# RMS norm with gelu: the squares, the gelu and the store of one group in a row on ScalarE

## The chip, the cores and the metric

The kernel runs on one core of one Trainium2 chip. The metric is device time in microseconds (us) of one execution, as the median of several. The profile is of one execution; its span is from the first to the last instruction.

Four engines matter: ScalarE (ACT in the profile; squares, gelu, and issue of the stores), VectorE (DVE; the product with gamma), GpSimd (POOL; the inverse root) and SyncE (SP; issue of the loads). TensorE only spreads gamma over the partitions at the start.

## The reference

```python
# x: 8 x 1024 x 2048, gamma: 2048, all float32
rms = np.sqrt(np.mean(x ** 2, axis=-1, keepdims=True) + eps)
out = gamma * x / rms
return 0.5 * out * (1 + np.tanh(np.sqrt(2 / np.pi) * (out + 0.044715 * out ** 3)))
```

The input is 67.1 MB, the output as much.

## The kernel before

The 8192 rows are cut into 16 groups; a group gives each of 128 partitions four rows, 4.19 MB in all. Six buffers ("slots") hold groups. A group is loaded into a slot, changed in place, and stored from it; the load of group g + 6 needs the store of group g to be done.

```python
ROWS = 4
SLOTS = 6
...
store_pieces = {G - 1: [(0, 2), (2, 2)]}
scale_pieces = {G - 1: [(0, 1), (1, 1), (2, 1), (3, 1)]}
...
def squares(g):                      # ScalarE, 4 x [128, 2048], sum per row
    for r in range(R):
        nc.scalar.activation(out=junk, in_=slot[g % SLOTS][:, r, :],
                             func=ACT.Square, accum_out=ssq[:, g, r : r + 1])

def scale(g):                        # VectorE, rows *= gamma
    for r, n in scale_pieces.get(g, [(0, R)]):
        rows = slot[g % SLOTS][:, r : r + n, :]
        nc.vector.tensor_tensor(out=rows, in0=rows, in1=gamma_ps..., op=ALU.mult)

def inverse_rms(g):                  # GpSimd, six small instructions -> rstd
    ...

def gelu_store(g):                   # ScalarE: gelu(rstd * row), then the store
    for r, n in store_pieces.get(g, [(0, R)]):
        for q in range(r, r + n):
            nc.scalar.activation(out=row, in_=row, func=ACT.Gelu_apprx_tanh,
                                 scale=rstd[:, g, q : q + 1])
        nc.scalar.dma_start(out=o3[g, :, r : r + n, :], in_=...)
...
for g in range(G + 1):
    if g < G:
        squares(g)
        inverse_rms(g)
        scale(g)
    if g:
        gelu_store(g - 1)
        if g - 1 + SLOTS < G:
            load(g - 1 + SLOTS)
```

The loop is shifted by one: ScalarE does the squares of group g, and then the gelu of group g - 1, whose scale and inverse root were made meanwhile by the other engines.

Of the kernel before, what the change touches and what calls it, by code (L numbers as in the profile page):

```python
# [1 line left out]

# [4 lines left out]

FP32 = mybir.dt.float32
ALU = mybir.AluOpType
ACT = mybir.ActivationFunctionType  # L10

P = 128
ROWS = 4
SLOTS = 6

GW = 128


@with_exitstack
def kernel(  # L20
    ctx: ExitStack,
    tc: tile.TileContext,
    x: bass.AP,
    gamma: bass.AP,
    eps: bass.AP,
    out: bass.AP,
):




    nc = tc.nc
    D = x.shape[-1]
    R = ROWS
    eps_f = float(eps)
    x3 = x.rearrange("b s d -> (b s) d").rearrange("(g p r) d -> g p r d", p=P, r=R)
    o3 = out.rearrange("b s d -> (b s) d").rearrange("(g p r) d -> g p r d", p=P, r=R)
    G = x3.shape[0]

    sbuf = ctx.enter_context(tc.tile_pool(name="sbuf", bufs=1))  # L40
    psum = ctx.enter_context(
        tc.tile_pool(name="psum", bufs=1, space=bass.MemoryType.PSUM)
    )
    slot = [sbuf.tile([P, R, D], FP32, name=f"slot{i}") for i in range(SLOTS)]
    gamma_row = sbuf.tile([1, D // GW, GW + 16], FP32, name="gamma_row")
    ones = sbuf.tile([1, P], FP32, name="ones")
    warm = sbuf.tile([1, 1], FP32, name="warm")
    power = sbuf.tile([P, R], FP32, name="power")
    ssq = sbuf.tile([P, G, R], FP32, name="ssq")
    rstd = sbuf.tile([P, G, R], FP32, name="rstd")  # L50
    ms = sbuf.tile([P, R], FP32, name="ms")
    y = sbuf.tile([P, R], FP32, name="y")
    z = sbuf.tile([P, R], FP32, name="z")
    gamma_ps = psum.tile([P, D], FP32, name="gamma_ps")
    junk = psum.tile([P, D], FP32, name="junk")

    store_pieces = {G - 1: [(0, 2), (2, 2)]}
    scale_pieces = {G - 1: [(0, 1), (1, 1), (2, 1), (3, 1)]}

    def load(g):  # L60
        nc.sync.dma_start(out=slot[g % SLOTS], in_=x3[g])  # L61

    def squares(g):
        for r in range(R):
            nc.scalar.activation(  # L65
                out=junk,
                in_=slot[g % SLOTS][:, r, :],
                func=ACT.Square,
                accum_out=ssq[:, g, r : r + 1],
            )  # L70

    def scale(g):
        for r, n in scale_pieces.get(g, [(0, R)]):
            rows = slot[g % SLOTS][:, r : r + n, :]
            nc.vector.tensor_tensor(  # L75
                out=rows,
                in0=rows,
                in1=gamma_ps.unsqueeze(1).to_broadcast([P, n, D]),
                op=ALU.mult,
            )  # L80

    def inverse_rms(g):

        v = nc.gpsimd
        v.tensor_scalar(  # L85
            out=ms, in0=ssq[:, g, :], scalar1=1.0 / D, scalar2=eps_f,
            op0=ALU.mult, op1=ALU.add,
        )
        v.tensor_tensor(out=y, in0=ms, in1=power, op=ALU.pow)  # L89
        v.tensor_tensor(out=z, in0=y, in1=y, op=ALU.mult)  # L90
        v.tensor_tensor(out=z, in0=z, in1=ms, op=ALU.mult)  # L91
        v.tensor_scalar(  # L92
            out=z, in0=z, scalar1=-0.5, scalar2=1.5, op0=ALU.mult, op1=ALU.add
        )
        v.tensor_tensor(out=rstd[:, g, :], in0=z, in1=y, op=ALU.mult)  # L95

    def gelu_store(g):
        for r, n in store_pieces.get(g, [(0, R)]):
            for q in range(r, r + n):
                row = slot[g % SLOTS][:, q, :]  # L100
                nc.scalar.activation(  # L101
                    out=row, in_=row, func=ACT.Gelu_apprx_tanh,
                    scale=rstd[:, g, q : q + 1],
                )
            nc.scalar.dma_start(  # L105
                out=o3[g, :, r : r + n, :], in_=slot[g % SLOTS][:, r : r + n, :]
            )

    with tc.manual_schedule():
        for g in range(SLOTS):  # L110
            load(g)
        nc.scalar.dma_start(
            out=gamma_row[:, :, 0:GW],
            in_=gamma.rearrange("(o a b) -> o a b", o=1, b=GW),
        )
        nc.gpsimd.memset(power, -0.5)  # L116
        nc.vector.memset(warm, 0.0)  # L117
        nc.vector.memset(ones, 1.0)  # L118
        nc.scalar.activation(out=warm, in_=warm, func=ACT.Gelu_apprx_tanh)  # L119
        for k in range(0, D, 512):  # L120
            nc.tensor.matmul(  # L121
                out=gamma_ps[:, k : k + 512],
                lhsT=ones,
                rhs=gamma_row[:, k // GW : (k + 512) // GW, 0:GW],
                start=True,
                stop=True,
            )
        for g in range(G + 1):
            if g < G:
                squares(g)  # L130
                inverse_rms(g)
                scale(g)
            if g:
                gelu_store(g - 1)
                if g - 1 + SLOTS < G:
                    load(g - 1 + SLOTS)


# [1 line left out]
_INS = ['x', 'gamma', 'eps']  # L140
_OUTS = [((8, 1024, 2048), 'float32')]

_NUMBERS = {'eps': 9.999999747378752e-06}


# [26 lines left out]
```

## Time and profile before

| | before |
|---|---|
| time, median of 4 runs | 317.65 us |
| span of the profile (of an execution that took 318.66 us) | 316.9 us |
| ScalarE busy | 251.1 us (79%) |
| VectorE busy | 139.4 us (44%) |
| DMA, mean rate | 424 GB/s |
| ScalarE waits for loads | 43.7 us |
| ScalarE waits for VectorE or GpSimd | none |

The chain of the kernel before, that is, the work that ended last followed backwards to what released it, by engine and then by line, as shares of the span ("issue" is time in which the engine waited for nothing that the profile shows; ACTq and SPq are the instruction queues of ScalarE and SyncE, the issue of transfers above all):

```profile
DMA 56%; ACT 33%; issue 5%; ACTq 1%; SPq 0%
DMA slot<-in_x_dram 30%; DMA out_dram<-slot 26%; ACT slot L101 19%; ACT junk L65 14%; ACTq L105 1%; SPq L61 0%; ACTq L101 0%; ACTq L65 0%
```

More than half of this chain is transfers, loads and stores. No instruction of VectorE or GpSimd is in it.

### The profile page before, as it was taken

What the parts mean: (1) busy time and instruction counts of PE and PEld (TensorE: products, weight loads), DVE (VectorE), ACT (ScalarE), POOL (GpSimd) and SP (SyncE); (2) the same over time, 40 slices, a digit from 0 to 9 for tenths busy, and PEclk for the clock granted to TensorE, in tenths of its full rate; (3) what the DMA queues carried; (4) which work ended last, traced back from release to release, by engine and by line L of the source; (5) the groups of instructions that cost most, each with busy time, mean ns of one, the idle gap of its engine ahead of it and who ended that gap; (6) DMA issues with size and microseconds to landing.
All of it is one profiled execution on the core that took longest, in us unless ns stands there. A gap on an engine that the chain in (4) does not pass through costs nothing.

```text
span 316.9 us, 473 instructions
## 1 busy us (share of the span) xinstructions
PE 7.2 (2%) x8; PEld 2.5 (1%) x8; DVE 139.4 (44%) x21; ACT 251.1 (79%) x194; POOL 32.3 (10%) x101
## 2 busy tenths in 40 slices
PE   0900000000000000000000000000000000000000
PEld 0300000000000000000000000000000000000000
DVE  0038909090919191732808246091550905582000
ACT  1379999999999997959689595995959859599800
POOL 0020102020202020202002020020200102001000
DMA  8999999999999999999999999999999999999995
GB/s 328 414 451 426 434 393 459 401 459 402 459 405 455 426 434 431 430 434 426 438 426 455 410 455 418 443 426 430 434 430 435 422 459 405 459 414 447 422 420 230
DMA packets 4787, 134.25 MB, mean 424 GB/s; under 512 B 544, under 2 KB 560, under 8 KB 560
## 3 DMA queue, kind: packets, MB, share of 16 engines
q1 hardware_dynamic: 2304, 67.11, 49.5%
q10 hardware_dynamic: 2480, 67.12, 49.1%
q14 instruction: 3, 0.02, 0.0%
HBM read 67.12 MB, written 67.11 MB: 424 GB/s over the span
## 4 chain that ended last, share of the span: by engine, by line
DMA 56%; ACT 33%; issue 5%; ACTq 1%; SPq 0%
DMA slot<-in_x_dram 30%; DMA out_dram<-slot 26%; ACT slot L101 19%; ACT junk L65 14%; ACTq L105 1%; SPq L61 0%; ACTq L101 0%; ACTq L65 0%
## 5 line engine op out<-in xcount | busy, mean ns | idle before, releaser
L75 DVE TENSOR_TENSOR slot<-slot,gamma_ps 128x8192 f32<-128x8192 f32 (+1 forms) x19 | 139.2, 7340 | 147.0 <-ACT junk L65 147.0
L65 ACT ACTIVATE junk<-slot 128x2048 f32<-128x2048 f32 x64 | 120.4, 1881 | 47.3 <-DMA slot<-in_x_dram 43.7
L101 ACT ACTIVATE slot<-slot,rstd 128x2048 f32<-128x2048 f32 x64 | 122.8, 1989 | 0.9 <-ACT slot L101 0.9
L85 POOL TENSOR_SCALAR ms<-ssq 128x4 f32<-128x4 f32 x16 | 3.1, 194 | 247.5 <-ACT junk L65 247.5
L89 POOL TENSOR_TENSOR y<-ms,power 128x4 f32<-128x4 f32 x16 | 16.1, 1009 | 1.3
L65 ACT ACTIVATION_READ_ACCUMULATOR junk<-slot 128x1 f32 x64 | 12.0, 188 | 0.0
L121 PE MATMUL gamma_ps<-gamma_row,ones 1*128 1x512 f32 x8 | 7.2, 1072 | 8.4 <-DMA gamma_row<-in_gamma_dram 8.4
L95 POOL TENSOR_TENSOR rstd<-z,y 128x4 f32<-128x4 f32 x16 | 3.2, 201 | 1.3
L91 POOL TENSOR_TENSOR z<-z,ms 128x4 f32<-128x4 f32 x16 | 3.2, 201 | 1.3
L90 POOL TENSOR_TENSOR z<-y 128x4 f32<-128x4 f32 x16 | 3.2, 199 | 1.3
L92 POOL TENSOR_SCALAR z<-z 128x4 f32<-128x4 f32 x16 | 3.1, 194 | 1.4
L121 PEld LDWEIGHTS gamma_ps<-gamma_row,ones 1*128 1x128 f32 x8 | 2.5, 325 | 11.5 <-issue 11.5
L119 ACT ACT_TABLE_LOAD x1 | 1.3, 1283 | 1.3 <-PEq L153 1.3
L117 DVE MEMSET warm<- 1x1 f32 x1 | 0.1, 59 | 0.8 <-PEq L153 0.8
L119 ACT ACTIVATE warm<-warm 1x1 f32<-1x1 f32 x1 | 0.2, 202 | 0.0
L118 DVE MEMSET ones<- 1x128 f32 x1 | 0.2, 165 | 0.0
L116 POOL MEMSET power<- 128x4 f32 x1 | 0.1, 102 | 0.3 <-POOLq L153 0.3
L153 POOL MEMSET const-float32-0.0<- 128x1 f32 x1 | 0.1, 99 | 0.2 <-issue 0.2
L153 POOL MEMSET const-bfloat16-1.0<- 128x1 bf16 x1 | 0.1, 102 | 0.0
L153 POOL MEMSET const-uint8-127<- 128x1 uint8 x1 | 0.1, 102 | 0.0
L153 POOL MEMSET const-float32-1.0<- 128x1 f32 x1 | 0.1, 99 | 0.0
## 6 DMA issues: line engine op xcount, KB each, us to landing
slot<-in_x_dram SPq DMA_DIRECT2D x16, 4096.0 KB, 37.1
out_dram<-slot ACTq DMA_DIRECT2D x15, 4096.0 KB, 38.6
out_dram<-slot ACTq DMA_DIRECT2D x2, 2048.0 KB, 15.0
gamma_row<-in_gamma_dram ACTq DMA_DIRECT2D x1, 8.0 KB, 7.5
```

The costliest lines, as they stand in the source:

```text
L65: nc.scalar.activation(out=junk, in_=slot[g % SLOTS][:, r, :], func=ACT.Square, accum_out=ssq[:, g, r : r + 1],)
L75: nc.vector.tensor_tensor(out=rows, in0=rows, in1=gamma_ps.unsqueeze(1).to_broadcast([P, n, D]), op=ALU.mult,)
L85: v.tensor_scalar(out=ms, in0=ssq[:, g, :], scalar1=1.0 / D, scalar2=eps_f, op0=ALU.mult, op1=ALU.add,)
L89: v.tensor_tensor(out=y, in0=ms, in1=power, op=ALU.pow)
L90: v.tensor_tensor(out=z, in0=y, in1=y, op=ALU.mult)
L91: v.tensor_tensor(out=z, in0=z, in1=ms, op=ALU.mult)
L92: v.tensor_scalar(out=z, in0=z, scalar1=-0.5, scalar2=1.5, op0=ALU.mult, op1=ALU.add)
L95: v.tensor_tensor(out=rstd[:, g, :], in0=z, in1=y, op=ALU.mult)
L101: nc.scalar.activation(out=row, in_=row, func=ACT.Gelu_apprx_tanh, scale=rstd[:, g, q : q + 1],)
L105: nc.scalar.dma_start(out=o3[g, :, r : r + n, :], in_=slot[g % SLOTS][:, r : r + n, :])
L119: nc.scalar.activation(out=warm, in_=warm, func=ACT.Gelu_apprx_tanh)
L121: nc.tensor.matmul(out=gamma_ps[:, k : k + 512], lhsT=ones, rhs=gamma_row[:, k // GW : (k + 512) // GW, 0:GW], start=True, stop=True,)
```

## The change

The intent, as the code reads, is to finish a group at once: its squares, its gelu and its store follow each other on ScalarE, so that a slot is given back earlier. To keep the wait for the scale short, the scale is cut in two halves of two rows, each issued after the squares of its rows. This is done in groups 0 to 9 only, whose slots are used again; groups 10 to 15 have one scale of four rows. The finer pieces of the last group's scale and store go, and two memsets move from VectorE to GpSimd.

```diff
-    def scale(g):
-        for r, n in scale_pieces.get(g, [(0, R)]):
-            rows = slot[g % SLOTS][:, r : r + n, :]
+    def scale(g, r, n):
+        rows = slot[g % SLOTS][:, r : r + n, :]
...
-    def gelu_store(g):
-        for r, n in store_pieces.get(g, [(0, R)]):
+    def gelu(g):
+        for r in range(R):
...
+    def store(g):
+        nc.scalar.dma_start(out=o3[g], in_=slot[g % SLOTS])
...
-        nc.vector.memset(warm, 0.0)
-        nc.vector.memset(ones, 1.0)
+        nc.gpsimd.memset(warm, 0.0)
+        nc.gpsimd.memset(ones, 1.0)
...
-        for g in range(G + 1):
-            if g < G:
-                squares(g)
-                inverse_rms(g)
-                scale(g)
-            if g:
-                gelu_store(g - 1)
-                if g - 1 + SLOTS < G:
-                    load(g - 1 + SLOTS)
+        for g in range(G):
+            n = HALF if g < G - SLOTS else R      # HALF = 2
+            for r in range(0, R, n):
+                squares(g, r, n)
+                scale(g, r, n)
+            inverse_rms(g)
+            gelu(g)
+            store(g)
+            if g + SLOTS < G:
+                load(g + SLOTS)
```

More of the change, by code (lines that the diff above doesn't have):

```diff
@@ L14 @@
 SLOTS = 6
+HALF = 2
 GW = 128
@@ L55, with squares @@
     junk = psum.tile([P, D], FP32, name="junk")
-    store_pieces = {G - 1: [(0, 2), (2, 2)]}
-    scale_pieces = {G - 1: [(0, 1), (1, 1), (2, 1), (3, 1)]}
     def load(g):
         nc.sync.dma_start(out=slot[g % SLOTS], in_=x3[g])
-    def squares(g):
-        for r in range(R):
+    def squares(g, r, n):
+        for q in range(r, r + n):
             nc.scalar.activation(
                 out=junk,
-                in_=slot[g % SLOTS][:, r, :],
+                in_=slot[g % SLOTS][:, q, :],
                 func=ACT.Square,
-                accum_out=ssq[:, g, r : r + 1],
+                accum_out=ssq[:, g, q : q + 1],
             )
-    def scale(g):
-        for r, n in scale_pieces.get(g, [(0, R)]):
-            rows = slot[g % SLOTS][:, r : r + n, :]
-            nc.vector.tensor_tensor(
-                out=rows,
-                in0=rows,
-                in1=gamma_ps.unsqueeze(1).to_broadcast([P, n, D]),
-                op=ALU.mult,
-            )
+    def scale(g, r, n):
+        rows = slot[g % SLOTS][:, r : r + n, :]
+        nc.vector.tensor_tensor(
+            out=rows,
+            in0=rows,
+            in1=gamma_ps.unsqueeze(1).to_broadcast([P, n, D]),
+            op=ALU.mult,
+        )
     def inverse_rms(g):
@@ L95, in inverse_rms @@
         v.tensor_tensor(out=rstd[:, g, :], in0=z, in1=y, op=ALU.mult)
-    def gelu_store(g):
-        for r, n in store_pieces.get(g, [(0, R)]):
-            for q in range(r, r + n):
-                row = slot[g % SLOTS][:, q, :]
-                nc.scalar.activation(
-                    out=row, in_=row, func=ACT.Gelu_apprx_tanh,
-                    scale=rstd[:, g, q : q + 1],
-                )
-            nc.scalar.dma_start(
-                out=o3[g, :, r : r + n, :], in_=slot[g % SLOTS][:, r : r + n, :]
-            )
+    def gelu(g):
+        for r in range(R):
+            row = slot[g % SLOTS][:, r, :]
+            nc.scalar.activation(
+                out=row, in_=row, func=ACT.Gelu_apprx_tanh,
+                scale=rstd[:, g, r : r + 1],
+            )
+    def store(g):
+        nc.scalar.dma_start(out=o3[g], in_=slot[g % SLOTS])
     with tc.manual_schedule():
```

## The prediction

> **What bounds the kernel now.** I read four views in this order: the page (busy shares, transfer rate), the waits of ScalarE, the groups by form for durations, and the timeline of one group for the order on each engine.
>
> The page of the kernel before:
>
> ```profile
> PE 7.2 (2%) x8; PEld 2.5 (1%) x8; DVE 139.4 (44%) x21; ACT 251.1 (79%) x194; POOL 32.3 (10%) x101
> ...
> DMA  8999999999999999999999999999999999999995
> GB/s 328 414 451 426 434 393 459 401 459 402 459 405 455 426 434 431 430 434 426 438 426 455 410 455 418 443 426 430 434 430 435 422 459 405 459 414 447 422 420 230
> DMA packets 4787, 134.25 MB, mean 424 GB/s; under 512 B 544, under 2 KB 560, under 8 KB 560
> ```
>
> The DMA row is full from the second slice to the last but one. The transfers are the bound: 134.25 MB at 424 GB/s is the whole span of 316.9 us. No compute engine is above 79%. A group of 4 rows moves 4.19 MB in and 4.19 MB out; at the 433 GB/s that the windows between 80 and 240 us show, that is 19.4 us a group, and the timeline has the first squares of successive groups at 140.10, 159.44 and 178.78 us, 19.34 apart.
>
> The waits of ScalarE:
>
> ```profile
> ACT junk L65 <- DMA slot<-in_x_dram: 43.7, 11, 10.3
> ACT junk L65 <- ACT slot L101: 2.1, 5, 0.4
> ```
>
> ScalarE waits for loads (43.7 us), and never for VectorE or GpSimd: no such line is in the view. The slack is smaller than 21% idle suggests. Before about 119 us it has none: it works off the loads that came early, one group in 16.1 us. After that it has 3.7 us in each 19.34.
>
> The groups by form, then the timeline around group 0, the only place where a group's sums and its scale stand with nothing before them:
>
> ```profile
> L75 DVE TENSOR_TENSOR slot<-slot,gamma_ps 128x8192 f32<-128x8192 f32 x15 | 130.3, 8688 | 142.4 <-ACT junk L65 142.4
> L101 ACT ACTIVATE slot<-slot,rstd 128x2048 f32<-128x2048 f32 x64 | 122.8, 1989 | 0.9 <-ACT slot L101 0.9
> L65 ACT ACTIVATE junk<-slot 128x2048 f32<-128x2048 f32 x64 | 120.4, 1881 | 47.3 <-DMA slot<-in_x_dram 43.7 <-ACT slot L101 2.1
> L89 POOL TENSOR_TENSOR y<-ms,power 128x4 f32<-128x4 f32 x16 | 16.1, 1009 | 1.3
> ```
>
> ```profile
> 13.13 1.88 ACT L65 ACTIVATE junk<-slot 128x2048 f32<-128x2048 f32 x1 [10.29 <-DMA slot<-in_x_dram]
> ...
> 21.05 0.19 ACT L65 ACTIVATION_READ_ACCUMULATOR junk<-slot 128x1 f32 x1
> 21.27 8.69 DVE L75 TENSOR_TENSOR slot<-slot,gamma_ps 128x8192 f32<-128x8192 f32 x1 [20.27 <-ACT junk L65]
> 21.33 0.20 POOL L85 TENSOR_SCALAR ms<-ssq 128x4 f32<-128x4 f32 x1 [20.51 <-ACT junk L65]
> ...
> 22.91 1.88 ACT L65 ACTIVATE junk<-slot 128x2048 f32<-128x2048 f32 x1 [1.67 <-DMA slot<-in_x_dram]
> ...
> 23.55 0.20 POOL L95 TENSOR_TENSOR rstd<-z,y 128x4 f32<-128x4 f32 x1
> ...
> 30.93 7.67 ACT L101 ACTIVATE slot<-slot,rstd 128x2048 f32<-128x2048 f32 x4
> ...
> 38.62 0.36 ACTq L105 DMA_DIRECT2D out_dram<-slot  x1
> 39.03 1.88 ACT L65 ACTIVATE junk<-slot 128x2048 f32<-128x2048 f32 x1 [0.43 <-ACT slot L101]
> ```
>
> The reader is to see three things. Four squares take 13.13 to 21.24, 8.11 us. The scale follows 0.03 us later and takes 8.69; the inverse root ends at 23.75, 2.51 us after the squares. And ScalarE does the squares of group 1 (22.91 on) while VectorE scales group 0: that is what hides the 8.69 us.
>
> **What the Trainium skill says.** (1) "ScalarE: Activation LUTs", section "What ACT_TABLE_LOAD costs": an activation with immediate scale and bias takes 186 ns plus 0.833 ns an element, each pointer operand about 93 ns more, and back-to-back ones overlap by about 93 ns. At 2048 elements that is 1892 and 1985; the trace has 1881 and 1989, and four gelus in 7.67, so 1.89 apart. It agrees. (2) "VectorE: DVE Perf Modes", section on the TRN2 errata: a 32-bit tensor by tensor operation takes (N+151)/0.96 ns. For 8192 that is 8690, the trace has 8688. For the new 4096 form, which no row shows, it gives an estimate of 4.42 us. (3) "DMA: Bandwidth & Descriptors", section "Issuing engines are not separate DMA queues": transfers issued by different engines run on the same 16 DMA engines and interleave. The trace agrees: loads and stores share one 433 GB/s. (4) "Perfetto Trace Analysis", section "Optimization Strategy" under "Identifying Performance Opportunities": a kernel can have regimes with different limits. The trace shows that for this one (16.1 us a group of ScalarE first, 19.34 of DMA later), and I argue that the change makes a third.
>
> **The change part by part.** The compiled order of instructions shows the ScalarE stream as four squares, four gelus, store, group by group; the first gelu of a group waits for VectorE and GpSimd. Groups 0 to 9 have two scales of 128x4096, groups 10 to 15 one of 128x8192. ScalarE takes instructions in order, so a gelu that waits holds back the next group's squares.
>
> *Groups 0 to 9.* Squares 8.11. The first scale half runs beside squares 3 and 4 (4.42 against 4.07, it ends about 0.4 after them). The inverse root ends 2.51 after the squares; with about 0.08 for the signal the first gelu starts 2.59 after them. The second half queues behind the first, some 4.8 to 4.9 us after the squares; the third gelu would start at 2.59 + 3.79 = 6.4, so it waits for nothing. Four gelus 7.67, then 0.43 from the last gelu's end to the next squares (38.60 to 39.03). Sum 8.11 + 2.59 + 7.67 + 0.43 = 18.80 us of ScalarE a group.
>
> *Groups 10 to 15.* The one scale starts only after all four squares: 8.11 + 0.03 + 8.69 + 0.08 + 7.67 + 0.43 = 25.01 us.
>
> One small addition: the compiled program has the fourth gelu of each group wait on ScalarE's own semaphore, which it did not before. In the squares such a wait makes the next start 0.02 after the former ended instead of overlapping, so I allow 0.12: 18.9 and 25.1.
>
> *What lies beside other work.* 18.9 us is just under the 19.4 of the DMA, but the early loads are already there: the sixth load lands near 80 us before, while ScalarE starts group 5 only at 13.1 + 5 x 18.9 = 107.6. With reads and writes halving the DMA, a load lands each 19.4 us after the third, against 18.9 of use: the lead of 18 us shrinks by 0.5 a group and lasts through group 10. So ScalarE never waits for a load, and its chain sets the end: 13.13 (first load) + 10 x 18.9 + 6 x 25.1 = 352.7, less 0.4 for the issue in the sum, so the last store is issued near 352.3. The removed split of the last store counts too: the last 4.19 MB now go alone, nothing queued ahead. The first load took 12.4 us from issue to landing, the same size; 2.1 lie between the last landing and the end before (300.64 + 14.2 to 316.9). So span 352.3 + 12.4 + 2.1 = 366.8, and the timed median stands 1.0 above the profile's span (317.9 to 316.9): 367.8. I take 367.5.
>
> *The memsets* that move to GpSimd cost 0.2 us beside the 8.4 us wait for gamma: nothing.
>
> **The rivals.** (a) *The transfers still hide all.* The full DMA row and 21% idle on ScalarE speak for it, and stores go out earlier after their load. Against it: 16 groups of over 18.8 us serial work are at least 301 us plus 13 before and 14 after. This would be about 318. (b) *Only the length of 18.9 matters*, as if whole scales in the last six cost nothing because no slot is reused there: 13.1 + 16 x 18.9 + 14.5 + 1 = 331, slower by 4%. The compiled order speaks against it, since in-order gelus wait for the whole scale. (c) *The early gelu waits for both halves* through a coarse wait: first groups would take 8.11 + about 4.9 + 7.67 + 0.43 = 21.1 us, above the DMA's pace, and the end some 22 us later, 390. The compiled order has separate waits for gelu one and three, so it is unlikely. (d) *Store issues on ScalarE block* on a semaphore shared with an older transfer: the waits are on stores four groups back or on a load that landed long before; at worst a few us.
>
> **Range and chances.** The sum is of measured durations and the order is fixed; the doubts are 16 small gaps (0.1 each, 2 us), the lone last store (2 us) and the early groups (2 us). Range 362 to 373. Faster 0.01, same 0.02, slower 0.97.
>
> **What would show it.** The waits of ScalarE should have gelu on VectorE, about 6 x 8.8 = 53 us (last six), gelu on GpSimd, about 10 x 2.6 = 26 us, and for loads only the first 10 us. First squares should be 18.9 apart to group 10, then 25.1. The DMA row should thin out in the last third. If squares still wait for loads in the middle, the DMA share was misjudged and the time is longer in that stretch; if the last groups stand less than 20 us apart, the step on in-order waits is wrong and the time is near 331.

## The result, and the profile after

The changed kernel takes 363.8 us (median of 4 runs, 363.73 to 364.11) against 317.65 us for the kernel before in the same rounds. The ratio is 1.1443, with a 95% interval of 1.1402 to 1.1483: slower by 14%. Ratios here are the mean time of one kernel's fast runs over that of the other's of the same rounds, so not quite the ratio of the medians quoted.

The page of the changed kernel: busy time of the engines, then the busy share of the DMA in tenths and its rate in 40 slices of 9.05 us each.

```profile
PE 7.2 (2%) x8; PEld 2.5 (1%) x8; DVE 139.7 (39%) x26; ACT 252.5 (70%) x194; POOL 32.3 (9%) x103
...
DMA  8999999999999999999999999999998508209028
GB/s 345 409 460 402 413 445 424 442 427 434 435 431 438 427 442 417 453 413 449 413 456 413 453 416 453 416 453 416 445 421 351 232 0 348 116 29 434 0 116 348
DMA packets 4643, 134.25 MB, mean 371 GB/s; under 512 B 528, under 2 KB 544, under 8 KB 544
```

The engines do the same work as before: ScalarE 252.5 us against 251.1, VectorE 139.7 against 139.4. The bytes are the same too. What differs is the last quarter: for 30 slices the transfers run as before, and then they thin out, with whole slices idle. In the window from 40 to 200 us the changed kernel moved 433 GB/s, the one before 432. In the window from 201 to 351 us it moved 298.

The chain by engine, and the waits of ScalarE (engine and group, what it waited for: us in total, times, longest):

```profile
ACT 65%; DVE 14%; issue 6%; POOL 6%; DMA 3%; ACTq 1%
```

```profile
ACT slot L98 <- DVE slot L73: 52.9, 6, 8.8
ACT slot L98 <- POOL rstd L93: 25.2, 10, 2.5
ACT junk L64 <- DMA slot<-in_x_dram: 10.3, 1, 10.3
```

Of the transfers only 3% is left in the chain: the first load. VectorE and GpSimd are in it now. Before, ScalarE waited 43.7 us in 11 waits for loads and never for these two. Now it waits for one load only, the first, but 78.1 us for the two engines: six times 8.8 us for VectorE and ten times 2.5 us for GpSimd. Its idle time before did not go away; it was replaced by another wait and grew.

The timeline of group 1, one of the first ten (start, duration, engine, line, operation; in brackets the idle time before it and what ended it):

```profile
31.87 1.88 ACT L64 ACTIVATE junk<-slot 128x2048 f32<-128x2048 f32 x1 [0.43 <-ACT slot L98]
...
35.94 8.75 DVE L73 TENSOR_TENSOR slot<-slot,gamma_ps 128x4096 f32<-128x4096 f32 x2 [9.99 <-ACT junk L64]
...
39.79 0.19 ACT L64 ACTIVATION_READ_ACCUMULATOR junk<-slot 128x1 f32 x1
...
42.27 0.20 POOL L93 TENSOR_TENSOR rstd<-z,y 128x4 f32<-128x4 f32 x1
42.50 7.68 ACT L98 ACTIVATE slot<-slot,rstd 128x2048 f32<-128x2048 f32 x4 [2.52 <-POOL rstd L93]
50.21 0.34 ACTq L104 DMA_DIRECT2D out_dram<-slot  x1
50.59 1.88 ACT L64 ACTIVATE junk<-slot 128x2048 f32<-128x2048 f32 x1 [0.42 <-ACT slot L98]
```

From squares to squares it is 50.59 - 31.87 = 18.72 us. The scale halves end at 44.69, while the first two gelus run. What ScalarE waits for is the last of GpSimd's six instructions, which ends at 42.47. Compare the kernel before, where ScalarE went from the squares into the gelu of the former group without a gap.

The timeline of group 10, the first with a whole scale:

```profile
208.22 0.19 ACT L64 ACTIVATION_READ_ACCUMULATOR junk<-slot 128x1 f32 x1
208.44 8.69 DVE L73 TENSOR_TENSOR slot<-slot,gamma_ps 128x8192 f32<-128x8192 f32 x1 [14.03 <-ACT junk L64]
...
217.22 7.67 ACT L98 ACTIVATE slot<-slot,rstd 128x2048 f32<-128x2048 f32 x4 [8.82 <-DVE slot L73]
224.93 0.34 ACTq L104 DMA_DIRECT2D out_dram<-slot  x1
225.32 1.88 ACT L64 ACTIVATE junk<-slot 128x2048 f32<-128x2048 f32 x1 [0.42 <-ACT slot L98]
```

The whole scale lies between the squares and the gelu, with both sides waiting for it. The squares of group 10 start at 200.31, so this group takes 25.01 us, and so do the five after it. The last store is issued at 349.97 and lands 11.1 us later.

### The profile page after: what moved, and what is told of

It reads as the page before. It is cut to its first block, busy times and chain, and to the rows that moved or that the text cites. A ratio compares the mean times of both kernels' runs of the same rounds, so it can differ in the third digit from the quotient of the medians.

```text
span 362.1 us, 483 instructions
## 1 busy us (share of the span) xinstructions
PE 7.2 (2%) x8; PEld 2.5 (1%) x8; DVE 139.7 (39%) x26; ACT 252.5 (70%) x194; POOL 32.3 (9%) x103
## 2 busy tenths in 40 slices
DMA packets 4643, 134.25 MB, mean 371 GB/s; under 512 B 528, under 2 KB 544, under 8 KB 544
## 4 chain that ended last, share of the span: by engine, by line
ACT 65%; DVE 14%; issue 6%; POOL 6%; DMA 3%; ACTq 1%
ACT junk L64 36%; ACT slot L98 30%; DVE slot L73 14%; DMA slot<-in_x_dram 3%; POOL y L87 3%; ACTq L104 1%; POOL z L89 1%; POOL rstd L93 1%; POOL z L88 1%; POOL z L90 1%; POOL ms L83 1%; ACTq L98 0%
## 5 line engine op out<-in xcount | busy, mean ns | idle before, releaser
L73 DVE TENSOR_TENSOR slot<-slot,gamma_ps 128x4096 f32<-128x4096 f32 (+1 forms) x26 | 139.7, 5403 | 202.5 <-ACT junk L64 202.5
L98 ACT ACTIVATE slot<-slot,rstd 128x2048 f32<-128x2048 f32 x64 | 122.8, 1989 | 78.1 <-DVE slot L73 52.9
L64 ACT ACTIVATE junk<-slot 128x2048 f32<-128x2048 f32 x64 | 120.4, 1881 | 18.0 <-DMA slot<-in_x_dram 10.3
## 6 DMA issues: line engine op xcount, KB each, us to landing
slot<-in_x_dram SPq DMA_DIRECT2D x16, 4096.0 KB, 53.1
```

Source lines behind the costliest of these rows:

```text
L64: nc.scalar.activation(out=junk, in_=slot[g % SLOTS][:, q, :], func=ACT.Square, accum_out=ssq[:, g, q : q + 1],)
L73: nc.vector.tensor_tensor(out=rows, in0=rows, in1=gamma_ps.unsqueeze(1).to_broadcast([P, n, D]), op=ALU.mult,)
```

## The experiments

The theory: ScalarE takes instructions in order, so each group's path is a sum of its squares, the wait for the slower of GpSimd and VectorE, its gelus and its store issue. Groups 0 to 9 pay GpSimd's chain, groups 10 to 15 the whole scale. On ScalarE no group overlaps with the next, and it never catches up with the loads, so the sum sets the end. The main rivals are that the transfers or the slots set the time (the stores come at other times now), and that the lone last store or the smaller scales cost a part.

All experiments gave right results and were timed in three rounds beside the kernel before, which stood at 317.3 to 317.5 us in each set. The diffs are shortened: "..." marks a cut, statements joined by ";" stand on lines of their own in the code, and "(half or whole)" stands for the loop over the pieces.

| run | edit | median us | ratio to before (95% interval) |
|---|---|---|---|
| the change | | 363.8 | 1.1443 (1.1402 to 1.1483) |
| e1_half_all | half scales in all groups | 326.15 | 1.0277 (1.0262 to 1.0293) |
| e2_order_alone | before, order alone changed | 417.02 | 1.3141 (1.3119 to 1.3163) |
| e3_order_undone | changed, order alone undone | 318.17 | 1.0026 (1.0000 to 1.0052) |
| e4_four_slots | changed, 4 slots | 364.05 | 1.1472 (1.1455 to 1.1489) |
| e5_two_inverse | changed, inverse root twice | 388.70 | 1.2242 (1.2222 to 1.2263) |
| e6_two_inverse_before | before, inverse root twice | 317.51 | 1.0009 (0.9988 to 1.0029) |
| e7_half_all_split_tail | e1 with the last store split | 322.56 | 1.0162 (1.0147 to 1.0177) |
| e8_last_six_undone | groups 10 to 15 in the old order | 322.51 | 1.0155 (1.0135 to 1.0176) |
| e9_first_ten_undone | groups 0 to 9 in the old order | 347.23 | 1.0935 (1.0919 to 1.0952) |

Differences under 2% count as "same": so e3, e6, e7 and e8. The intervals of e7 and e8 leave out 1, so their small losses are taken as real.

### e1_half_all: what the whole scales in the last six groups cost

```diff
-            n = HALF if g < G - SLOTS else R
+            n = HALF
```

> The changed kernel with two half scales in all 16 groups, also the last six. Theory (ScalarE's serial chain sets the end; in the last six groups the gelu waits for the whole 8.69 us scale): all groups 18.72 us apart, last store issued at 13.1 + 16 x 18.72 - 0.4 = 312.2 us, 11.1 to its landing, 1.0 to the end, 1.7 from span to time: about 326. Rival (the last six groups are slow because the DMA or the lone last store is): near 364, unchanged.

Measured: 326.15 us. Of the 46.2 us lost, 363.8 - 326.15 = 37.7 are the whole scales of the last six groups: 6 x (25.01 - 18.72) = 37.7. The waits of ScalarE:

```profile
ACT slot L98 <- POOL rstd L93: 40.5, 16, 2.5
ACT junk L64 <- DMA slot<-in_x_dram: 10.1, 1, 10.1
```

The wait for VectorE is gone altogether and all 16 groups wait 2.5 us for GpSimd. The last store was issued at 312.21, where the sum had it at 312.2. The rival falls: neither the DMA nor the lone store made the last six groups slow.

### e2_order_alone: the order without the half scales

```diff
-        for g in range(G + 1):
-            if g < G:
-                squares(g); inverse_rms(g); scale(g)
-            if g:
-                gelu_store(g - 1)
-                if g - 1 + SLOTS < G: load(g - 1 + SLOTS)
+        for g in range(G):
+            squares(g); inverse_rms(g); scale(g)
+            gelu_store(g)
+            if g + SLOTS < G: load(g + SLOTS)
```

> The kernel before with the order of the loop alone changed: squares, inverse root, whole scale, gelu and store of one group in a row. Theory: 15 groups of 25.01 us, the last with its four scale pieces and two stores some 18.8, so about 13.1 + 375.2 + 18.8 + 6.2 + 2.7 = 416 us. Rival (transfers hide most of it, because stores start sooner after their loads): below 340.

Measured: 417.02 us. The waits of ScalarE show where it comes from:

```profile
ACT slot L101 <- DVE slot L75: 132.2, 15, 8.8
...
ACT slot L101 <- POOL rstd L95: 2.5, 1, 2.5
```

Fifteen groups wait for a whole scale; the last, with its four scale pieces, waits only 2.5 us for GpSimd. So the new order would cost 99.7 us on the kernel as it was (417.02 against 317.29 in the same rounds). The change has only 46 us of it left. The half scales in ten groups save 6.3 us each, 63 in all, but dropping the finer pieces of the last group gives about 10 back: from its first squares to the end of the span it is 26.7 us in e2 and 36.8 in the changed kernel.

### e3_order_undone: everything of the change but the order

```diff
-        for g in range(G):
-            (half or whole) squares(g, r, n); scale(g, r, n)
-            inverse_rms(g)
-            gelu(g); store(g)
-            if g + SLOTS < G: load(g + SLOTS)
+        for g in range(G + 1):
+            if g < G:
+                (half or whole) squares(g, r, n); scale(g, r, n)
+                inverse_rms(g)
+            if g:
+                gelu(g - 1); store(g - 1)
+                if g - 1 + SLOTS < G: load(g - 1 + SLOTS)
```

> The changed kernel with the order alone undone: the squares of the following group again stand before the gelu of a group; the half scales, the one last store and the memsets on GpSimd stay. Theory: as the kernel before, 318 us, within 2 us, since the last store would be issued at the same place and the DMA has a backlog. Rival (the half scales or the unsplit last store cost a part of the 46 us): 325 or more.

Measured: 318.17 us, within 0.5% of before by its interval. The half scales, the unsplit last store and the moved memsets cost nothing that matters when the order is the old one. The whole loss needs the order. ScalarE's waits are back to those of the kernel before:

```profile
ACT junk L64 <- DMA slot<-in_x_dram: 43.6, 11, 10.1
...
ACT slot L98 <- DVE slot L73: 1.2, 1, 1.2
```

The 1.2 us are the last group's scale, which before was cut finer.

### e4_four_slots: are slots or transfers in it?

```diff
-SLOTS = 6
+SLOTS = 4
...
-            n = HALF if g < G - SLOTS else R
+            n = HALF if g < 10 else R
```

> The changed kernel with four buffers for groups instead of six (half scales still in groups 0 to 9). Theory (loads land well ahead of ScalarE; neither buffers nor transfers bound it): 364 us, within 3, and ScalarE waits for a load only at the start. Rival (the time is set by when stores free buffers for loads): ScalarE shows waits for loads in the middle and the time rises by 10 us or more.

Measured: 364.05 us, the same as the changed kernel, with two slots fewer. ScalarE's waits are the same line by line (52.9 us for VectorE, 25.2 for GpSimd, 10.3 for the first load). The median time from the issue of a load to its landing fell from 53.1 to 24.6 us: I read this as loads that, with six slots, only wait longer in the queue. In the changed kernel the early return of slots, the intent of the change, has nothing to act on.

### e5_two_inverse and e6_two_inverse_before: is GpSimd on the path?

```diff
             inverse_rms(g)
+            inverse_rms(g)
```

The same line was added to the changed kernel (e5) and to the kernel before (e6).

> The changed kernel with the inverse root computed twice in a row in every group (same result). Theory: GpSimd's chain is on the path in groups 0 to 9 and hidden behind the 8.69 us scale in groups 10 to 15, so ten times 2.45 us more: about 388. Rival 1 (GpSimd is off the path, the gaps are made up elsewhere): 364. Rival 2 (it counts in all groups): 403.

> The kernel before with the inverse root computed twice in a row in every group. Theory: a group's gelu comes after 8.1 us of the next group's squares, so 5 us of GpSimd stay hidden: 318, the same within 1%, except a few us at the very end at most (the last group has no next squares, but four gelus of the group before stand there). Rival (GpSimd's chain counts here too): 16 x 2.45 = 39 us more.

Measured: 388.70 us for e5, 24.9 more than the changed kernel's 363.8; 317.51 us for e6, the same as before. In e5, the waits of ScalarE are

```profile
ACT slot L98 <- DVE slot L73: 52.9, 6, 8.8
ACT slot L98 <- POOL rstd L93: 50.1, 10, 5.0
```

The ten waits for GpSimd went from 2.5 to 5.0 us each, and the six waits for VectorE did not change. So 32.1 us more work for GpSimd (64.4 against 32.3 busy) cost 24.9 us in the changed kernel, all of it in the first ten groups, and nothing in the kernel before, where the squares of the next group cover it. No run made the chain shorter, so what a faster one would win is not shown.

### e7_half_all_split_tail: the lone last store

The kernel of e1, with the last group's gelus and store in two pieces of two rows.

```diff
...
-            gelu(g)
-            store(g)
+            if g < G - 1:
+                gelu(g); store(g)
+            else:
+                for r in range(0, R, HALF):
+                    gelu(g, r, HALF); store(g, r, HALF)
```

> The changed kernel with half scales in all groups and the last group's store split in two pieces of two rows, each right after its gelus. Theory: last piece of 2 MB issued near 312.7 us, 6.2 to its landing (half of the bytes, 4.9 us less than 11.1), 2.7 to the end of the time: about 321.5, so 4.5 under the version with one last store. Rival (the DMA has a backlog at the end, so that the split gives nothing): as that version, 326.

Measured: 322.56 us, 3.6 under e1 where 4.5 were expected. The direction holds: here, at the end of a serial chain, the DMA has no backlog, so halving the last store counts (the two pieces took 6.6 us to land as the median, the whole store of e1 11.1). The same split is worth nothing in the old order (e3 has it unsplit and is as fast as before). This is the best version of the new order that was tried, still 1.6% slower than before.

### e8_last_six_undone and e9_first_ten_undone: do the two stretches add up?

```diff
-        for g in range(G):
+        def first(g):                 # the body before: squares, scale, inverse root
...
+        def second(g):                # gelu, store, next load
...
+        held = None
+        for g in range(G):
+            first(g)
+            if held is not None: second(held)
+            held = g
+            if g < G - SLOTS:         # e9: if g >= G - SLOTS - 1
+                second(g); held = None
+        if held is not None: second(held)
```

In e9, group 9 is the seam: its gelu follows that of group 8 and comes before the squares of group 10.

> The changed kernel with groups 0 to 9 in a row and, from group 10, the order of before (squares of the following group ahead of the gelu). Theory: in the first ten groups the transfers stay full at 433 GB/s, so nothing is lost for good; the last six catch up to the loads: 318 to 322. Rival (each serial group costs its own gap): 10 x 2.5 us of the 46 stay, 343.

> The changed kernel with groups 0 to 9 in the order of before and groups 10 to 15 in a row with whole scales. Theory: squares of group 10 start near 183.7 us instead of 200.3, then 6 x 25.01, less 0.4, 12.1 from the last store to the end and 1.7 to the time: 347. Rival (the last six alone make all of the loss, at whatever time they start): 364.

Measured: 322.51 us for e8 and 347.23 for e9. The sum for e9 was met. In e8 the ten serial groups at the start cost 5.1 us, not the 25.2 us of their waits: when the last six groups go back to the old order, ScalarE catches up and waits for loads again. Its waits, the first load's 10.2 us among them:

```profile
ACT slot L98 <- POOL rstd L93: 25.2, 10, 2.5
ACT junk L64 <- DMA slot<-in_x_dram: 21.2, 4, 10.2
```

The remaining 5.1 us put e8 just above the expected range. Its timeline shows the squares of the last group starting at 283.28 us after a wait for the load, against 276.24 in the kernel before: the last load came 7 us later. The traces show why. e8 and e3 differ in the order of the first ten groups alone, and in e3 these squares start at 276.08. Up to the last load, the DMA moved 429 GB/s in e8 and in the kernel before: that is 118.5 MB in 276.2 us before and 121.5 MB in 283.2 us in e8. The loads are the same 67.1 MB, so 3.0 MB more of stores had gone ahead of the last load, 7 us of transfer. The stores of the first ten groups came earlier (the first at 31.5 us instead of 38.6) and took their share of the DMA from the loads. After that load e8 had less left to move and the DMA thinned out: 338 GB/s to the end, against 389 before.

So the losses of the two stretches don't add. The ten early groups alone cost 5.1 us of their 25.2 us of waits (e8), the six late ones alone 29.8 (347.23 against 317.4) of their 53.2 (e9), and both together 46: undoing the first ten alone wins 16.6 us, undoing the last six alone 41.3, both together 45.6. The first ten groups make ScalarE start group 10 late, with slack that it could still recover; the last six then leave no chance to.

No version beats the kernel before. It keeps the DMA full from the second slice to the last but one, and the runs offer nothing that would move fewer bytes.

## Why the prediction was right

| step | predicted | measured |
|---|---|---|
| time | 367.5 (362 to 373) | 363.8 |
| groups 0 to 9, squares to squares | 18.9 | 18.72 |
| groups 10 to 15 | 25.1 | 25.01 |
| ScalarE waits for VectorE | 53, in the last six | 52.9, six times |
| ScalarE waits for GpSimd | 26, in the first ten | 25.2, ten times |
| ScalarE waits for loads | the first only | the first only, 10.3 |
| scale of 128x4096 | 4.42 | 4.418 |
| last store issued at | 352.3 | 349.97 |
| issue of the last store to the end of the span | 14.5 | 12.1 |
| time less span | 1.0 | 1.7 |

**Which regime.** The step that decided the sign was that the slack of ScalarE before was the DMA's doing, and that 16 serial groups, with the first load and the last store outside them, are longer than the DMA's whole work. The trace and e4 confirm it: no load is waited for after the first, with six slots and with four, and the groups alone take 10 x 18.72 + 6 x 25.01 = 337 us where 134.25 MB at 433 GB/s take 310. The two ends matter: in e1 the groups are only 16 x 18.72 = 299.5 us, less than the DMA's 310, and it is still slower, since the 13.0 us before the first squares and the 12.2 us after the last store's issue overlap with none of them.

**The scales in the last six groups.** The prediction took the program's order and concluded that a gelu behind a whole scale holds back all that follows. e1 shows that this is worth 37.7 us and removes the wait with one line. Its rival (b), that only the length of the first groups matters, had 331 for a kernel without that cost; the kernel that really has none took 326.15.

**GpSimd on the path.** The prediction put 2.5 us of each of the first ten groups on GpSimd and none of the last six. e5 doubled the chain and moved exactly those ten waits.

**The small terms.** The sum came out at 367.8 and the time at 363.8. Three terms differ. The allowance of 0.12 us in each group for a fourth gelu that waits on ScalarE's own signal was wrong: four gelus took 7.67 to 7.68 us in both kernels. With the slightly shorter gap after GpSimd (2.52 where 2.59 was assumed) it makes up the 2.3 us by which the last store was issued earlier. The end after the last store was set too long, since it was taken from a load at the start (12.4 us to landing) and from the end of a kernel whose DMA still had a backlog; a lone store of the same size landed after 11.1 us and 1.0 us later the span ended: 2.4 us less. And the time stood 1.7 us above the span instead of 1.0: the prediction set the median of other executions (317.9) against the span of the profiled one, which itself took 318.66, 1.8 us more than its span. In sum 367.8 - 2.3 - 2.4 + 0.7 = 363.8.

**The rivals.** Rival (a), transfers that hide all, would have been right for the first 200 us, where the DMA ran at 433 GB/s as before. It fell on what came after. Rival (c), a coarse wait for both halves, would have shown waits for VectorE in the first ten groups; there are none. Rival (d), store issues that block, would have lengthened the 0.42 us between gelu and squares; it is the same in both kernels.

## What to carry to other kernels

An engine with idle time is not free to be serialised: ask what fills the time between two dependent steps of one item, for here it was the next item's squares that hid 8.7 us of VectorE and 2.5 us of GpSimd, and an in-order engine that loses such work waits out the full latency. Splitting a step helps only where its latency is on the path, so it must be split in the last items too: that the slots of the last groups are not used again was no reason to leave those groups whole. Earlier stores gave nothing here: the transfers were already full, and in e8 the stores only pushed the loads back. And where a serial stretch stands counts: the early one cost 5.1 us of its 25.2 us of waits, since later work could still catch up, the late one 29.8 of 53.2.

## What the Trainium skill lacked or had wrong

- "DMA: Bandwidth & Descriptors", section "Where 436 GB/s comes from", says without a condition that the HBM side, about 358 GB/s, binds transfers between HBM and SBUF. With loads and stores mixed on one core, 433 GB/s were held here from 40 to 200 us, close to the single-core figure of 425 of the same page. That page's own note gives about 358 for each of two cores that stream at once; the runs here used one core.
- "VectorE: DVE Perf Modes", the section on the TRN2 errata, checks its formula for the 32-bit tensor by tensor addition at 512 and 2048 elements only. It held for the multiplication here at 4096 (4.418 us measured, 4.424 by formula) and 8192 (8.688 and 8.690), with the second operand in PSUM, which the section does not say.
- "ScalarE: Activation LUTs" gives no cost for a sum taken along with an activation. The read of the sum is an instruction of 0.19 us here, and squares start 2.03 us apart at a duration of 1.88.
- "DMA: Bandwidth & Descriptors", section "Issuing engines are not separate DMA queues", calls the time of the issue usually small relative to the transfer. That holds here (in the changed kernel 0.34 us of issue, 11.1 us or more to landing), but the section does not count what it takes from an engine that also computes: each store opened 0.42 us between the gelu and the next squares, 15 times on the path, 6.2 us in all, and the extra store of e7 opened the same 0.42 us between two gelus.
